# One branch in place of two around the last pair of experts

## The chip, the cores and the metric

The kernel runs on one core of one Trainium2 chip. The metric is the time of one execution on the device in microseconds (us), lower is better. The core has five engines, each with an instruction stream of its own: TensorE (PE in the profile, its weight loads PEld), VectorE (DVE), ScalarE (ACT), GpSimd (POOL) and SyncE (SP), which here only issues DMAs. The engines wait for each other through semaphores: every engine has a counter that its instructions raise, and others wait until it has reached a value.

## The reference

Two layers over 512 tokens of 1024 channels. Each layer is a mixer (layer 0: two convolution modules; layer 1: a gating unit and chunked attention), a layer norm, a mixture of experts and a second layer norm. The mixture is what matters here:

```python
# 32 experts (4 groups of 8); a token takes its best group, and the two best experts of it
expert_idx = g_idx * EXPERTS_PER_GROUP + e_idx          # (512, 2)
# each expert, on the tokens that chose it:
hb = jax.nn.silu(xb @ w_gate[e]) * (xb @ w_up[e])       # 1024 -> 512
y  = hb @ w_down[e]                                     # 512 -> 1024
# out: the two experts' results per token, weighted
```

How many tokens choose an expert depends on the data, so the kernel has code for every case and branches at run time over what isn't needed.

## The kernel before, in words

**Pairs.** `experts` (L977) goes over the 32 experts of a layer in 16 pairs (g = 0 to 15, L1056). A pair's tokens sit in 128 slots, 64 for each expert (or 96 and 32 in some pairs). For each pair PE computes the gate product (`proj2("g")`, L1063), ACT its Silu (`gated`, L755), PE the up product (`proj2("u")`, L1108), DVE the product of both (`hidden`, L760); PE transposes it and ACT copies the transposed tile `hT` to SBUF (`hidden_T`, L768); PE then computes the down product in two halves of 512 columns (`down`, L777, PSUM tiles `y0` and `y1`), from which ACT and DVE make two parts (L778, L779). The result of a pair is added to the tokens by `combine` (L789, L790 on PE, L798 on DVE) during the next pair. All expert products are issued by the helper line L745.

**Weights.** An expert has 6 MB of weights. SP streams them through eight large buffers ("units") and one more made of pieces, in an order fixed by `Stream` (L909): 2 MB matrices, each load waiting until PE has released the unit. The last pair's up and down weights are loaded as halves (L944, L947).

**Overflow.** Where an expert has more tokens than slots, two things can follow. `overflow` (L1079) handles a small excess of the pair with 128 slots more; it stands in a branch behind `hidden_T` (L1120, `tc.If(v > 0)`, v being the pair's count, loaded into registers at L1106 by all engines). `crowded` (L1031), the general loop, handles any number of tokens: for each of the 16 pairs it has a loop that gathers 64 tokens per expert, loads the six weight matrices into units (`slots`, L1032) and computes all of it. All 16 loops stand inside one branch (L1033, `tc.If(most > 0)`, most being the largest count of all pairs, loaded at L1128 at the end of pair 14). `crowded()` is called at the start of pair 15, ahead of its gate product (L1060).

An engine that doesn't enter a branch's body jumps over it, and then raises the semaphores by what the body would have raised them: these are the rows `EVENT_SEMAPHORE` of L1033 and L1120. Whoever uses a buffer after the branch that the body also uses waits for these raises. For PE alone a hint ahead of the branch (L1107, L1129) says which way it will go.

**After the branch of the last pair.** `last()` (L1061) is, in layer 0, `last0` (L1570): it loads the two 2 MB weights `val` and `v` of layer 1's mixer into units 7 and 3, which are also the two units that the general loop uses. `last2()` (L1124) is there `last0b` (L1575), which loads three more 2 MB weights and the 2 MB table TB behind it. In layer 1 `last()` is empty and `last2()` loads two rows of parameters. After the last pair's down halves follows `Last` (L800), which adds the result and takes the statistics of the layer norm.

Of the kernel before, what the change touches and what calls it, by code (L numbers as in the profile page):

```python
# [7 lines left out]
F32 = mybir.dt.float32  # L8
F32R = mybir.dt.float32r
BF = mybir.dt.bfloat16  # L10
I32 = mybir.dt.int32
AF = mybir.ActivationFunctionType
OP = mybir.AluOpType
AX = mybir.AxisListType
# [8 lines left out]
NP = NE // 2  # L23
# [3 lines left out]
COLS = [0, 1, 2, 3, 13, 4, 5, 12, 6, 7, 14, 8, 9, 15, 10, 11]  # L27
HEAVY = 12
NTHR = 6
WIDE = 3  # L30
# [13 lines left out]
def trunk(ctx: ExitStack, tc: tile.TileContext, a, out, layers=2, moe=True):  # L44
    nc = tc.nc
    PE, ACT, DVE, POOL = nc.tensor, nc.scalar, nc.vector, nc.gpsimd
# [3 lines left out]
    wk = ctx.enter_context(tc.tile_pool(name="wk", bufs=1))  # L50
# [3 lines left out]
    TT = DVE.tensor_tensor  # L54
# [11 lines left out]
    def small(shape, name, dt=F32, **kw):  # L66
        return wk.tile([128] + list(shape), dt, name=name, **kw)
# [374 lines left out]
    class Router:  # L442
# [178 lines left out]
        def counts(self):  # L621
            c = self.rk[:, NT]
            big = wk.tile([128, NE, NE], F32, name="big", tag="xb")
            TT(big, self.at, bc(c[:, None, :], [NE, NE]), op=OP.mult)
            cs = small([NP, 2], "cs", tag="rcb")
            DVE.tensor_reduce(cs.rearrange("p g two -> p (g two)"), big, axis=AX.X, op=OP.add)
            over = small([2, NP, 2], "over", tag="scr")
            for i in range(2):
                TT(over[:, i], cs, lim[:, i], op=OP.is_gt)
            nxs = small([2 * NP + 1], "nxs")  # L630
            n, m = nxs[:, 0:NP], nxs[:, NP:2 * NP]
            mxc = small([NP], "mxc", tag="mxc")
            DVE.tensor_reduce(mxc, over[:, 1], axis=AX.X, op=OP.max)
            DVE.scalar_tensor_tensor(n, over[:, 0, :, 1], 2.0, over[:, 0, :, 0], op0=OP.mult, op1=OP.add)
            DVE.scalar_tensor_tensor(n, mxc, float(WIDE), n, op0=OP.mult, op1=OP.max)
            mxe = small([NP], "mxe", tag="mxc")
            DVE.tensor_reduce(mxe, c.rearrange("p (g two) -> p g two", two=2), axis=AX.X, op=OP.max)
            nx = small([NP, NTHR], "nx", tag="scr")
            TT(nx, bc(mxe[:, :, None], [NP, NTHR]), bc(thr[:, None, :], [NP, NTHR]), op=OP.is_gt)
            DVE.tensor_reduce(m, nx, axis=AX.X, op=OP.add)  # L640
            for g in FIRST:
                DVE.scalar_tensor_tensor(m[:, g:g + 1], mxe[:, g:g + 1], float(CAP), m[:, g:g + 1], op0=OP.is_gt, op1=OP.add)
            DVE.tensor_reduce(nxs[:, 2 * NP:], m, axis=AX.X, op=OP.max)
            nxi = small([2 * NP + 1], "nxi", I32)
            DVE.tensor_copy(nxi, nxs)
            return nxi

# [99 lines left out]
    def proj2(tag, xt, wa, wb, own=EVEN[0]):  # L747
        p = ptile(tag)
        for k in range(KD):
            by_slots(p, xt[:, k], (wa[:, k], wb[:, k]), own, start=(k == 0), stop=(k == KD - 1))  # L750
        return p
# [6 lines left out]
    def hidden(sg, pu):  # L758
        h = wk.tile([128, 512], F32, name="h", tag="q1")
        DVE.tensor_mul(h, sg, pu)  # L760
        return h

    def hidden_T(h):
        p = mtile((128, 4, 128))
        for j in range(4):
            PE.transpose(p[:, j], h[:, j * 128:(j + 1) * 128], ident)  # L766
        hT = wk.tile([128, 4, 128], F32, name="hT", tag="q2")
        ACT.activation(hT, p, AF.Copy)  # L768
        return hT

# [11 lines left out]
    def onehot_S(tk, tag="q3"):  # L782
        S = wk.tile([128, T], F32R, name="S", tag=tag)
        TS(S, io, tk, None, op0=OP.is_equal)
        return S
# [6 lines left out]
    def combine(S, yh, yl, ts=range(NT)):  # L792
        for t in ts:
            for h in range(2):
                s = slice(h * 512, (h + 1) * 512)
                p = mtile()
                spread(p, S, yh, yl, t, h)
                DVE.tensor_add(acc[:, t, s], acc[:, t, s], p)  # L798
# [168 lines left out]
    ET = mybir.EngineType  # L967

    def count(nxi, i, **kw):
        return nc.values_load(nxi[0:1, i:i + 1], min_val=0, max_val=NTHR + 1,  # L970
                              skip_runtime_bounds_check_because="a count of blocks", **kw)

    def when(nxi, i, above, engines=None):
        v = count(nxi, i, **({} if engines is None else {"engines": engines}))
        return v, tc.If(v > above)

    def experts(rt, ws, T1, pt, x1d, xt, xg, xg2, update, last, last2, lead, finish):  # L977
# [52 lines left out]

        def crowded():  # L1031
            slots = ws.order[6:8]  # L1032
            with tc.If(most > 0, label=f"most{ws.l}", preferred_fallthrough_block=True):  # L1033
                for g in range(NP):
                    v, cond = when(nxi, NP + g, 0)
                    with cond:
                        cur = small([2, NT], "cur")
                        R3, yh, yl = (wk.tile([128, D], F32R, name="room", tag=t) for t in ("l1", "xt1", "lng"))
                        R3 = R3.rearrange("p (j t m) -> p j t m", j=2, t=NT)
                        TS(cur, rt.r, 0.0 if g in FIRST else -float(CAP), None, op0=OP.add)  # L1040
                        with tc.For_i(0, v, 1):
                            TS(cur, cur, -float(CAP), None, op0=OP.add)
                            rt.onehot(R3, range(NT), cur)
                            T3 = Table(rt, R3)
                            T3.one(2 * g)
                            gather(xg, x1d, T3.idx[:, 0:1])
                            xo = gather_T(xg, rt.gb, wk.tile([128, KD, 128], F32, name="xo", tag="xb"))
                            u = [ws.fetch(0, j, slots[j], g) for j in range(2)]
                            h3 = gated(proj2("g", xo, *u))
                            u = [ws.fetch(0, 2 + j, slots[j], g) for j in range(2)]  # L1050
                            h3 = hidden_T(hidden(h3, proj2("u", xo, *u)))
                            u = [ws.fetch(0, 4 + j, slots[j], g) for j in range(2)]
                            y3 = down(h3, *u, T3.wt[:, 0:1], (yh, yl))
                            combine(onehot_S(T3.tk[:, 0:1], "q2"), *y3)

        for g in range(NP):  # L1056
            W = lambda j: ws.u[6 * g + j]
            own, own2 = EVEN if COLS[g] < HEAVY else ODD
            if g == NP - 1:
                crowded()  # L1060
                last()  # L1061
            skip = f"skip{ws.l}_{g}"
            sg = gated(proj2("g", xt, W(0), W(1), own))  # L1063
            if g == 0:
# [14 lines left out]
            def overflow(v):  # L1079
                h2 = wk.tile([128, 512], F32, name="h2", tag="r")  # L1080
                xo = gather_T(xg2, rt.gb, wk.tile([128, KD, 128], F32, name="xo", tag="xb"))
                hT2 = wk.tile([128, 4, 128], F32, name="hT2", tag="q0")

                def wide():
                    ACT.activation(h2, proj8("g", xo, (W(0), W(1)), own2), AF.Silu)
                    DVE.tensor_mul(h2, h2, proj8("u", xo, (W(2), W(3)), own2))
                    hidden2_T(h2, hT2, 4)

                def single(e):
                    b = (0, 1) if own2 == EVEN[1] else (2, 1)  # L1090
                    s = slice(0, 128)
                    ACT.activation(h2[:, s], proj1("g", xo, W(e), b[e]), AF.Silu)
                    DVE.tensor_mul(h2[:, s], h2[:, s], proj1("u", xo, W(2 + e), b[e]))
                    hidden2_T(h2, hT2, 1)
                    r = slice(SUB * b[e], SUB * b[e] + SUB)
                    for i, src in enumerate((T2.tk, T2.wt)):
                        blocks4(tw, lambda o, c: DVE.tensor_copy(o[:, i:i + 1], col(src, g)[r]))
                either(v, wide, single)
                either(v, lambda: down8(hT2, (W(4), W(5)), col(T2.wt, g), col(T2.tk, g), own2),
                       lambda e: down1(hT2, W(4 + e), tw[:, 1:2], tw[:, 0:1]))  # L1100
# [2 lines left out]
                if g == NP - 1:  # L1103
                    combine(S, *prev, (0, 1))
            if g > 1:
                v = count(nxi, COLS[g])  # L1106
                tc.mark_branch_hint_location(skip, v > 0, engines=[ET.PE])  # L1107
            pu = proj2("u", xt, W(2), W(3), own)  # L1108
            h = hidden(sg, pu)
# [8 lines left out]
                combine(S, *prev, range(CM, NT))  # L1118
            if g > 1:
                with tc.If(v > 0, label=skip, preferred_fallthrough_block=True):  # L1120
                    overflow(v)
            ws.load(6 * g + 4 + 9)
            if g == NP - 1:
                last2()  # L1124
            if 0 < g < NP - 1:
                gather2(g + 1)
            if g == NP - 2:
                most = count(nxi, 2 * NP)  # L1128
                tc.mark_branch_hint_location(f"most{ws.l}", most > 0, engines=[ET.PE])  # L1129
            if g == NP - 1:  # L1130
                S = onehot_S(col(T1.tk, g))
            if g < NP - 1:
# [541 lines left out]
```

## Time and profile before

| | us |
|---|---|
| runs: median of 3 | 1455.97 |
| runs: lowest, highest | 1446.28, 1456.77 |
| the profiled execution, its own time | 1450.72 |
| the profiled execution, its span (first to last instruction) | 1448.9 |
| PE busy in the span | 1326.9 (92%) |
| DVE, ACT, POOL busy | 675.9, 368.3, 294.0 |
[...]

PE is busy nearly throughout, and the DMA queues move 420 GB/s and more while experts run, so two limits lie close together there. Layer 0's experts end and layer 1's mixer begins at about 700 us; layer 1's experts end at about 1430 us. A row of a group of instructions has its busy time, the mean of one in ns, the idle time of its engine just before, and what ended that idle time. A row of the timeline has the start, the length, the engine, the line, the operation, how many, and in brackets the idle time before it. Names that end in q (ACTq, DVEq, POOLq, SPq, PEldq) are instructions that the engine's sequencer handles by itself, such as branches and semaphore raises.

### The profile page before, as it was taken

Reading aid. Unit: us, or ns where it says so; the run is one execution under the profiler, and the core shown is the slowest. Engines: PE = TensorE matmul, PEld = TensorE weight load, DVE = VectorE, ACT = ScalarE, POOL = GpSimd, SP = SyncE. Lnnn points to the kernel's source line nnn. Section 1 sums busy time; section 2 is a strip of 40 time slices with the busy share of each in tenths; the row PEclk is TensorE's granted clock in tenths of the full one; section 3 lists DMA queues with packets and bytes.
Section 4 is the critical chain, followed back from the end, with each engine's and each line's share of the span. In section 5 each row is a group of like instructions: output and inputs, shape, how many; then the busy total and the mean of one; then the engine's idle time right before and its main releaser. Section 6 shows DMA issues by size and latency. Waiting matters only on the chain. (4 is left out here: it accounts for less than half of the span.)

```text
span 1448.9 us, 19205 instructions
## 1 busy us (share of the span) xinstructions
PE 1326.9 (92%) x7119; PEld 698.7 (48%) x7121; DVE 675.9 (47%) x1387; ACT 368.3 (25%) x694; POOL 294.0 (20%) x261
## 2 busy tenths in 40 slices
PE   9989999998978999988899999999998999988984
PEld 6767764343333433333576767744433343333331
DVE  7998588232222332232718555784322232322336
ACT  5545631111101111111524455521111111111101
POOL 5785610000000000000463229300000000000002
PEclk9999999999998999999999999999999999999997
DMA  7505479999997899999700018789999999999971
GB/s 293 232 5 241 166 262 425 420 424 422 420 400 301 355 426 423 422 420 378 283 1 1 23 66 325 268 320 423 421 423 424 423 423 422 425 421 422 420 304 59
DMA packets 56693, 461.19 MB, mean 318 GB/s; under 512 B 8661, under 2 KB 9301, under 8 KB 33089
## 3 DMA queue, kind: packets, MB, share of 16 engines
q1 hardware_dynamic: 51184, 449.96, 75.4%
q0 software_dynamic: 4464, 7.79, 1.5%
q8 instruction: 101, 1.65, 0.5%
q10 hardware_dynamic: 864, 1.13, 0.2%
q14 instruction: 80, 0.65, 0.1%
HBM read 461.04 MB, written 6.29 MB: 323 GB/s over the span
## 5 line engine op out<-in xcount | busy, mean ns | idle before, releaser
L745 PE MATMUL pu<-w,xt 128*64 128x512 f32 (+1 forms) x1280 | 247.8, 606 | 31.8 <-DMA w<-in_w_up_dram 31.8
L745 PE MATMUL py<-w,hT 128*64 128x512 f32 (+1 forms) x1280 | 242.3, 611 | 18.4 <-issue 7.3
L745 PE MATMUL pg<-w,xt 128*64 128x512 f32 (+1 forms) x1280 | 235.1, 600 | 10.9 <-ACTq L1033 10.9
L760 DVE TENSOR_TENSOR h<-sg,pu 128x512 f32<-128x512 f32 x32 | 22.0, 688 | 379.9 <-issue 342.7
L690 POOL DMA_INDIRECT xg<-x1d,idx x29 | 28.7, 990 | 794.3 <-PE m L439 711.6
L745 PEld LDWEIGHTS pu<-w,xt 128*64 128x64 f32 (+1 forms) x1280 | 75.4, 129 | 194.1 <-issue 149.0
L798 DVE TENSOR_TENSOR acc<-acc,m 128x512 f32<-128x512 f32 x240 | 148.6, 680 | 17.9 <-PE m L790 15.7
L745 PEld LDWEIGHTS pg<-w,xt 128*64 128x64 f32 (+1 forms) x1280 | 77.5, 127 | 163.4 <-issue 144.6
L745 PEld LDWEIGHTS py<-w,hT 128*64 128x64 f32 (+1 forms) x1280 | 71.7, 128 | 150.7 <-issue 146.8
L779 DVE SCALAR_TENSOR_TENSOR y<-py,wt,y 128x512 fp32r<-128x512 f32 x64 | 48.0, 750 | 194.6 <-ACT y L778 194.6
L778 ACT ACTIVATE y<-py,wt 128x512 fp32r<-128x512 f32 x64 | 44.0, 687 | 295.1 <-PE py L745 295.1
L789 PE MATMUL m<-y,S 128*128 128x512 f32 x248 | 106.2, 428 | 0.0
L109 POOL TENSOR_TENSOR wl<-win,wh 128x512 fp32r<-128x512 f32 x64 | 84.5, 1335 | 67.7 <-ACT wh L108 67.5
L790 PE MATMUL m<-y,S 128*128 128x512 f32 x248 | 97.8, 394 | 0.0
L768 ACT ACTIVATE hT<-m 128x512 f32<-128x512 f32 x32 | 19.1, 598 | 304.9 <-PE m L766 282.9
L109 POOL TENSOR_TENSOR wl<-wo,wh 128x512 fp32r<-128x512 f32 x64 | 82.3, 1314 | 34.8 <-ACT wh L108 34.4
L755 ACT ACTIVATE sg<-pg 128x512 f32<-128x512 f32 x32 | 19.1, 597 | 219.0 <-PE pg L745 219.0
L789 PEld LDWEIGHTS m<-y,S 128*128 128x128 f32 x248 | 46.6, 188 | 39.7 <-issue 26.9
L128 PE MATMUL m<-xh,wl 128*128 128x512 f32 x144 | 58.7, 408 | 3.1 <-POOL wl L109 3.1
L127 PE MATMUL m<-xh,wh 128*128 128x512 f32 x144 | 58.3, 405 | 0.8 <-ACT wh L108 0.8
L129 PE MATMUL m<-xl,wh 128*128 128x512 f32 x144 | 57.9, 402 | 0.0
L108 ACT ACTIVATE wh<-win 128x512 fp32r<-128x512 f32 x64 | 38.9, 625 | 49.0 <-PE pg L129 13.4
(445 smaller groups left out, 1858.8 us busy)
## 6 DMA issues: line engine op xcount, KB each, us to landing
w<-in_w_gate_dram SPq DMA_DIRECT2D x64, 2048.0 KB, 25.0
w<-in_w_up_dram SPq DMA_DIRECT2D x50, 2048.0 KB, 18.3
w<-in_w_down_dram SPq DMA_DIRECT2D x50, 2048.0 KB, 21.2
w<-in_w_up_dram SPq DMA_DIRECT2D x40, 512.0 KB, 24.7
w<-in_w_down_dram SPq DMA_DIRECT2D x40, 512.0 KB, 22.3
win<-in_w_in_dram SPq DMA_DIRECT2D x18, 512.0 KB, 7.6
wo<-in_w_out_dram SPq DMA_DIRECT2D x4, 2048.0 KB, 12.2
w<-in_w_up_dram SPq DMA_DIRECT2D x8, 1024.0 KB, 16.2
```

What stands on the lines that cost most here:

```text
L108: ACT.activation(h, src, AF.Copy)
L109: POOL.tensor_tensor(l, src, h, op=OP.subtract)
L127: PE.matmul(p, wh[:, j], xh[:, k], start=(k == 0), stop=False)
L128: PE.matmul(p, wl[:, j], xh[:, k], start=False, stop=False)
L129: PE.matmul(p, wh[:, j], xl[:, k], start=False, stop=(k == KD - 1))
L690: POOL.indirect_dma_start(out=dst, out_offset=None, in_=x1d, in_offset=bass.IndirectOffsetOnAxis(ap=idx_col, axis=0), bounds_check=T - 1, ...
L745: PE.matmul(p[w * c:w * c + w], x[:, w * c:w * c + w], ww[own[w * c // SUB]], **kw)
L778: ACT.activation(yh[:, s], p, AF.Copy, scale=wt)
L779: DVE.scalar_tensor_tensor(yl[:, s], p, wt, yh[:, s], op0=OP.mult, op1=OP.subtract)
L789: PE.matmul(p, S[:, t * 128:(t + 1) * 128], yh[:, s], start=start, stop=False)
L790: PE.matmul(p, S[:, t * 128:(t + 1) * 128], yl[:, s], start=False, stop=True)
L798: DVE.tensor_add(acc[:, t, s], acc[:, t, s], p)
```

## The change

The call of the general loop moves from the start of pair 15 into the body of that pair's overflow branch, behind the up product. The branch is now taken when either is needed: a 34th count, the sum of most and of the last pair's own count, is made on DVE in `counts` and loaded in place of the pair's own at L1106. Inside, each part has a branch of its own. The separate load of most at the end of pair 14, its hint, and the branch around the general loop ahead of the gate product go. Since `hT` of the last pair now lives across the general loop, the loop takes other buffers for its own hidden tile (`q3` in place of `q2`) and its one-hot matrix (`r` in place of `q2`). `last()` moves with the call, from ahead of the gate product to behind the branch.

```diff
@@ counts
-            nxs = small([2 * NP + 1], "nxs")
+            nxs = small([2 * NP + 2], "nxs")
...
-            DVE.tensor_reduce(nxs[:, 2 * NP:], m, axis=AX.X, op=OP.max)
-            nxi = small([2 * NP + 1], "nxi", I32)
+            DVE.tensor_reduce(nxs[:, 2 * NP:2 * NP + 1], m, axis=AX.X, op=OP.max)
+            TT(nxs[:, 2 * NP + 1:], nxs[:, 2 * NP:2 * NP + 1], n[:, COLS[-1]:COLS[-1] + 1], op=OP.add)
+            nxi = small([2 * NP + 2], "nxi", I32)
@@ hidden_T
-    def hidden_T(h):
+    def hidden_T(h, tag="q2"):
...
-        hT = wk.tile([128, 4, 128], F32, name="hT", tag="q2")
+        hT = wk.tile([128, 4, 128], F32, name="hT", tag=tag)
@@ count
-        return nc.values_load(nxi[0:1, i:i + 1], min_val=0, max_val=NTHR + 1,
+        return nc.values_load(nxi[0:1, i:i + 1], min_val=0, max_val=NTHR + 1 + WIDE,
@@ crowded
-            with tc.If(most > 0, label=f"most{ws.l}", preferred_fallthrough_block=True):
+            with when(nxi, 2 * NP, 0)[1]:
...
-                            h3 = hidden_T(hidden(h3, proj2("u", xo, *u)))
+                            h3 = hidden_T(hidden(h3, proj2("u", xo, *u)), "q3")
...
-                            combine(onehot_S(T3.tk[:, 0:1], "q2"), *y3)
+                            combine(onehot_S(T3.tk[:, 0:1], "r"), *y3)
@@ the loop over pairs
-            if g == NP - 1:
-                crowded()
-                last()
             skip = f"skip{ws.l}_{g}"
             sg = gated(proj2("g", xt, W(0), W(1), own))
...
-                v = count(nxi, COLS[g])
+                v = count(nxi, COLS[g] if g < NP - 1 else 2 * NP + 1)
                 tc.mark_branch_hint_location(skip, v > 0, engines=[ET.PE])
             pu = proj2("u", xt, W(2), W(3), own)
...
                 with tc.If(v > 0, label=skip, preferred_fallthrough_block=True):
-                    overflow(v)
+                    if g < NP - 1:
+                        overflow(v)
+                    else:
+                        v1, cond = when(nxi, COLS[g], 0)
+                        with cond:
+                            overflow(v1)
+                        crowded()
+                if g == NP - 1:
+                    last()
             ws.load(6 * g + 4 + 9)
...
-            if g == NP - 2:
-                most = count(nxi, 2 * NP)
-                tc.mark_branch_hint_location(f"most{ws.l}", most > 0, engines=[ET.PE])
```

## Rows read from the trace of the kernel before

**Rows 1.** The page's groups: line, operation xcount | busy, mean ns | idle before, releaser
```profile
L745 PE MATMUL pg<-w,xt 128*64 128x512 f32 (+1 forms) x1280 | 235.1, 600 | 10.9 <-ACTq L1033 10.9
```
**Rows 2.** Line 1033, both layers: operation xcount: ns min/median/max, first and last start
```profile
L1033 PEldq COMPARE_BRANCH  x2: 6067/6130/6194, 656.4 to 1383.9; - x2
L1033 ACTq COMPARE_BRANCH  x2: 45/45/45, 660.1 to 1387.6; - x2
L1033 ACTq EVENT_SEMAPHORE  x4: 17/17/17, 665.4 to 1393.1; - x4
L1033 SPq COMPARE_BRANCH  x2: 45/45/45, 668.5 to 1395.5; - x2
L1033 SPq EVENT_SEMAPHORE  x14: 17/17/17, 673.8 to 1405.0; - x14
```
**Rows 3.** Timeline, PE and ACT, last pair of layer 0 and then of layer 1
```profile
656.40 3.65 PE L745 MATMUL py<-w,hT 128*64 128x512 f32 x16
665.46 8.93 PE L745 MATMUL pg<-w,xt 128*64 128x512 f32 x32 [5.40 <-ACTq L1033]
676.38 7.09 PE L745 MATMUL pu<-w,xt 128*64 128x512 f32 x32
686.06 0.60 ACT L768 ACTIVATE hT<-m 128x512 f32<-128x512 f32 x1 [10.97 <-PEq L1120]
686.71 3.65 PE L745 MATMUL py<-w,hT 128*64 128x512 f32 x16 [0.74 <-ACTq L1120]
...
1393.08 8.64 PE L745 MATMUL pg<-w,xt 128*64 128x512 f32 x32 [5.54 <-ACTq L1033]
```
**Rows 4.** Timeline, PE, first down products of pairs 13 and 14 in layer 0
```profile
619.01 3.64 PE L745 MATMUL py<-w,hT 128*32 128x512 f32 x32
...
651.80 3.65 PE L745 MATMUL py<-w,hT 128*64 128x512 f32 x16 [0.80 <-PEq L1120]
```
**Rows 5.** Line 1120, last pair of layer 0, then all branches of PE and ACT
```profile
L1120 PEldq COMPARE_BRANCH  x1: 442/442/442, 684.9 to 684.9; - x1
L1120 ACTq COMPARE_BRANCH  x1: 45/45/45, 686.1 to 686.1; - x1
...
L1120 PEldq COMPARE_BRANCH  x28: 89/358/4182, 270.7 to 1412.3; - x28
L1120 ACTq EVENT_SEMAPHORE  x27: 17/17/17, 269.5 to 1414.0; - x27
```
**Rows 6.** Windows: A:B length, busy by engine, granted clock of PE, DMA share, GB/s
```profile
665.00:670.00 5.00, 4.54 (x14) 1.46 (x16) 0.48 (x1) 0.00 (x0) 0.00 (x0) 0.58 1.02 378
680.00:685.00 5.00, 5.00 (x25) 2.21 (x21) 1.42 (x3) 0.00 (x0) 0.00 (x0) 1.00 1.01 429
1405.00:1415.00 10.00, 9.26 (x46) 4.06 (x44) 3.56 (x6) 1.52 (x2) 0.00 (x0) 1.00 0.38 123
```
**Rows 7.** One load each, lines 964 (layer 1), 1573, 1331: issue, then us to landing
```profile
L964 SPq DMA_DIRECT2D w<-in_w_gate_dram x1: 333/333/333, 1362.2 to 1362.2; - x1
DMA to landing us min/median/max: 25.6/25.6/25.6
...
L1573 SPq DMA_DIRECT2D wval<-in_w_in1t_dram x1: 356/356/356, 675.2 to 675.2; - x1
DMA to landing us min/median/max: 9.8/9.8/9.8
...
L1331 SPq DMA_DIRECT2D row<-in_rows_dram x1: 363/363/363, 690.2 to 690.2; - x1
DMA to landing us min/median/max: 22.2/22.2/22.2
```
**Rows 8.** First readers of lines 1573's and 1331's loads: timeline ACT, then line 1360
```profile
698.36 1.14 ACT L108 ACTIVATE wh<-wval 128x512 fp32r<-128x512 f32 x2
...
L1360 DVE TENSOR_TENSOR val<-m,row x4: 673/684/692, 722.8 to 736.6; 128x512 f32<-128x512 f32 x4
```
**Rows 9.** Line 642 on DVE: a small operation of the shape of the added one
```profile
L642 DVE SCALAR_TENSOR_TENSOR nxs<-mxe,nxs x4: 152/156/159, 230.2 to 975.1; 128x1 f32<-128x1 f32 x4
```

## The prediction, made before the change was run

> **What bounds the kernel now.** I read the page's groups first. The gate product is idle ahead of itself for 10.9 us in all, and all of it is put down to ACT at line 1033, the branch around the general loop [rows 1]. With two layers that is some 5.4 us a layer, and it is the only thing that ever holds a gate product. Then I read line 1033 alone [rows 2]. The reader is to see that no engine goes into the body (each has a branch and then raises) and how far a branch and the first raise behind it lie apart: on ACT 660.1 to 665.4, on SP 668.5 to 673.8. Both take 5.3 us although the branch itself takes 45 ns; on PE the branch itself takes 6.07 and 6.19 us. So each engine pays this for itself, at full DMA load (share 1.02, [rows 6]). Third, the timeline of the last pair [rows 3]: the second down half of pair 14 ends at 656.40 + 3.65 = 660.05, and the gate product begins at 665.46, when ACT has raised its counter. PE's own branch was over by 656.4 + 6.07 = 662.5, so ACT's is the late one. [...] Fourth, line 1120, the overflow branch: the same jump, over a short body, costs ACT nothing that PE sees. In the last pair ACT's branch stands at 686.1 and PE goes on at 686.71, just after `hT` is copied (686.06 + 0.60 = 686.66) [rows 3, 5]. I read the 5.3 us as the fetch of instructions that aren't at hand after a long jump; that reading is a guess from the rows, the 5.3 us are not.
>
> Neither branch is taken in either layer's last pair: ACT makes 27 raises at line 1120 for 28 branches, the last at 1414.0, in layer 1's last pair [rows 5], and line 1033 has raises for both layers. The inputs are the same, so the sum of both counts is zero and the merged branch is skipped too.
>
> **The change part by part, layer 0.**
> (a) The load of most and its hint at the end of pair 14 go. They stand between PE's raise and its next weight load: PE is idle 0.80 us ahead of that pair's down product, in pair 13 too little to be shown [rows 4]. Minus 0.7 us.
> (b) The branch ahead of the gate product goes: minus 5.40 us of idle time [rows 3]. Late next would be the gate weights, but nothing held them here: the only releaser of gate products is line 1033 [rows 1].
> (c) With the stall goes the slow stretch behind it: 8.93 - 7.09 = minus 1.84 us [rows 3].
> (d) The merged branch has the general loop in its body, so it is the long jump that line 1033 was. PE's hint is for PE alone. ACT reaches the branch when it has issued `hT` (686.06 and 686.1 in the old times, [rows 3, 5]), and raises 5.3 us later. The down product writes `y0`, which the general loop's down product writes as well and ACT reads there; so PE must wait for that raise. Nothing covers it: between `hT` and the down product PE has no other work. Old: 686.71 - 686.06 = 0.65 us from `hT` to the down product. New: 5.25 to 5.4 for the jump (660.1 to 665.4, and 5.4 in layer 1 [rows 2]) and 0.08 for PE, 5.33. Plus 4.7 us. The bounds are 4.18 us, the longest that PE took at line 1120, and 6.19, its longest at line 1033 [rows 2, 5]; below stands also nothing at all, if the jump should find its target at hand (a rival). I take 5.3, the row of the same engine and the same body. PE's own branch, some 1.1 us ahead of `hT` (684.9 against 686.06), would end 5.0 us behind `hT` even if its hint came to nothing: not the later one.
> (e) The slow stretch then follows this stall, in the down product: plus 1.84, by (c).
> Sum: -0.7 - 5.4 - 1.84 + 4.7 + 1.84 = -1.4 us.
>
> **Layer 1.** The second gate weight was issued at 1362.2 and lands 25.6 us later, 1387.8 [rows 7]; so (a) gives nothing and the gate product starts at 1387.8 in place of 1393.08: -5.28 [rows 3]. (c) and (e) cancel again (8.64 - 7.09 = 1.55 each). (d) is +4.8, with 5.4 on ACT. Sum -0.5 us. By then the DMA queues are at a share of 0.38 (1405 to 1415, [rows 6]), which may shorten the fetch.
>
> [...] No run here shows a long jump over idle queues.
>
> **What costs nothing.** One operation more on DVE in each layer, 0.16 us by its neighbour [rows 9], in pair 0, where the first user of the counts is two pairs on; if it weren't covered, 0.3 us in all. The other tags: the general loop doesn't run. The one-hot matrix behind the branch takes `q3` and so waits for the raises too, but it is needed only after 3.65 us of down product. `last()` and `last2()`: SP reaches the old branch at 668.5 and the two loads go out at 675.2 [rows 2, 7]. SP still jumps from about 668.5 to 673.8, but units 7 and 3 are used by the general loop, whose raise on PE now comes with the merged branch: PE's branch moves from 684.9 to 684.9 - 7.9 = 677.0 (the sum of a to c), and with 6.1 us of jump the raise is at 683.2. The loads leave 8 us later, and everything behind them in a queue that is full (1.01 from 680 to 685, [rows 6]) moves by up to as much. Their readers: `val` landed at 675.2 + 9.8 = 685.0 and is first read at 698.36, later 693 against 697. The row of biases issued at 690.2 landed at 712.4 and is read at 722.8; later 720.4 against 721.4 [rows 7, 8]. So it just fits, with 1 us to spare at the worst, and I take nothing.
>
> **The sum.** -1.4 - 0.5 = -1.9 us. Against the profiled execution's own time, 1450.72 (span 1448.9 and 1.8 around it), that is 1448.8. The three timed runs went from 1446.28 to 1456.77 with a median 5.25 above the profiled one; the mean of these four is 1452.4, so for a new median I forecast 1452.4 - 1.9 = 1450.5.
>
> **Rivals.**
> First, the stall doesn't come back: the target of the merged jump is at hand, or the raise isn't waited for. For it: 27 jumps of ACT at line 1120 cost nothing. Against it: those bodies are short, and at line 1033 both engines shown, in both layers, paid at least 5.3 us. Then (d) and (e) fall away: -7.9 and -5.28 - 1.55 = -6.8, together -14.7: 1437.7, 1.0% less.
> Second, slower: the loads of `last()` are held so long that layer 1's mixer waits. That decides from the point where the row of biases lands after 721.4, that is, when the loads leave more than 9 us late. If SP pays a second jump of 5.3 us behind PE's raise, they leave at 683.2 + 5.3 = 688.5, 13.3 us late; the row lands at 725.7, 4.3 us after it is wanted, and the whole is 2.4 us slower: 1454.8. Against it: SP waits for nobody ahead of its own branch at line 1033, and jumps while PE is still busy.
> Third, layer 1's code lies elsewhere in memory, and PE's hinted branches, 0.36 us at the median and 4.18 once in 28 [rows 5], miss more often. Each miss costs up to 3.8 us; two of them make 1456.2.
> That the change doesn't do what it says would need a count above zero, which the rows exclude.
>
> **Chances and range.** Forecast 0.66, first rival 0.1, second 0.11, third 0.13. A measurement of this kernel tells about 1% (14.5 us) from no change. The first rival lies on that bound, so half of it is faster; the others are within. Since runs of one kernel here lie 10 us apart, I leave 0.03 for slower and 0.07 for faster. The range is the bounds of (d) in both layers (1448 to 1452), widened by the spread of runs, 5 us to either side, and by the second and third rival above and part of the first below: 1442 to 1459.
>
> **What would show it.** Right: in both layers the gate product of the last pair follows the down half with no idle time and takes 7.1 us; the down product stands idle some 5.4 us before it, put down to ACT at line 1120, and takes about 1.8 us longer than 3.65; ACT's branch and raise at line 1120 lie 5.3 us apart in the last pair; the loads of line 1573 leave at about 683. Wrong: no gap at line 1120 (first rival), a DMA or DVE `val` wait in layer 1's mixer (second), or PE branches of 4 us at other pairs of layer 1 (third).

## The result, and the profile after

The changed kernel takes 1444.61 us at the median of 20 runs (1440.08 to 1451.12), the kernel before 1454.05 us at the median of 20 runs beside it (1446.28 to 1457.83). The medians are 9.4 us apart and the means 7.7; the ratio taken from all these runs is 0.995, with an interval of 0.9936 to 0.9964: some 7 us faster, where 1.9 us were forecast. The profiled execution took 1445.25 us (span 1443.1). Run twice more, in other sessions, the same kernel gave 0.994 (0.9916 to 0.9964) and 0.9954 (0.9932 to 0.9976).

The page's groups come first; this line answers to [rows 1]:

```profile
L746 PE MATMUL pg<-w,xt 128*64 128x512 f32 (+1 forms) x1280 | 232.7, 594 | 0.1
```

The gate products, 10.9 us idle before, now never wait at their start. The wait has gone to the down product, and it is smaller. The timeline of PE at the last pair, layer 0 and then layer 1, answers to [rows 3] and, with its first line, to [rows 4]:

```profile
644.23 3.65 PE L746 MATMUL py<-w,hT 128*64 128x512 f32 x16
648.84 3.65 PE L746 MATMUL py<-w,hT 128*64 128x512 f32 x16
652.33 8.12 PE L746 MATMUL pg<-w,xt 128*64 128x512 f32 x32
662.43 7.09 PE L746 MATMUL pu<-w,xt 128*64 128x512 f32 x32
675.71 5.35 PE L746 MATMUL py<-w,hT 128*64 128x512 f32 x16 [3.68 <-DVEq L1118]
...
1382.95 8.13 PE L746 MATMUL pg<-w,xt 128*64 128x512 f32 x32
...
1406.56 5.35 PE L746 MATMUL py<-w,hT 128*64 128x512 f32 x16 [3.89 <-DVEq L1118]
```

Three things are to be seen. The gate product follows pair 14's down product at once in both layers. It takes 8.12 us, 1.03 more than the up product. The down product stands idle 3.68 and 3.89 us ahead of itself, not 5.4, and what releases it is DVE at the merged branch (now L1118), not ACT; then it runs 1.70 us longer than the 3.65 of its kind.

Who jumps how long is seen at line 1118 alone, in layer 0 and in layer 1. These answer to [rows 2] and [rows 5]: a branch and the first raise behind it are one engine's jump.

```profile
L1118 PEldq EVENT_SEMAPHORE  x2: 51/51/51, 672.1 to 672.2; - x2
L1118 ACTq EVENT_SEMAPHORE  x2: 17/17/17, 674.9 to 675.0; - x2
L1118 DVEq EVENT_SEMAPHORE  x2: 21/21/21, 675.4 to 675.5; - x2
...
L1118 PEldq COMPARE_BRANCH  x1: 342/342/342, 671.0 to 671.0; - x1
L1118 DVEq COMPARE_BRANCH  x1: 56/56/56, 671.6 to 671.6; - x1
L1118 ACTq COMPARE_BRANCH  x1: 45/45/45, 672.1 to 672.1; - x1
...
L1118 ACTq EVENT_SEMAPHORE  x2: 17/17/17, 1405.7 to 1405.8; - x2
L1118 DVEq EVENT_SEMAPHORE  x2: 21/21/21, 1406.3 to 1406.4; - x2
...
L1118 DVEq COMPARE_BRANCH  x1: 56/56/56, 1402.3 to 1402.3; - x1
L1118 ACTq COMPARE_BRANCH  x1: 45/45/45, 1402.7 to 1402.7; - x1
```

ACT's jump took 2.9 and 3.0 us, DVE's 3.8 and 4.0; before, at line 1033, ACT's took 5.3 and 5.4 [rows 2] and DVE's 5.6 and 5.5. PE's branch took 0.34 us, where the one at line 1033 had taken 6.07. The windows around the jump show what else differs (columns as in [rows 6]):

```profile
670.00:672.00 2.00, 2.00 (x11) 1.45 (x9) 2.00 (x4) 0.00 (x0) 0.00 (x0) 1.00 0.19 71
672.00:674.00 2.00, 0.03 (x1) 0.00 (x0) 0.72 (x2) 0.60 (x1) 0.00 (x0) 1.00 0.74 157
676.00:680.00 4.00, 4.00 (x12) 1.36 (x10) 0.25 (x1) 0.57 (x2) 0.00 (x0) 0.57 1.00 414
1401.00:1403.00 2.00, 1.67 (x10) 1.16 (x8) 2.00 (x4) 0.29 (x1) 0.00 (x0) 1.00 0.13 49
1403.00:1405.00 2.00, 0.00 (x0) 0.00 (x0) 0.36 (x1) 0.30 (x1) 0.00 (x0) 1.00 0.09 28
```

and those of the kernel before around its jumps at line 1033:

```profile
660.00:665.00 5.00, 0.06 (x2) 0.00 (x0) 0.75 (x1) 0.69 (x1) 0.00 (x0) 0.74 1.00 399
1388.00:1393.00 5.00, 0.00 (x0) 0.00 (x0) 0.75 (x1) 0.30 (x1) 0.00 (x0) 0.98 1.01 391
```

Before, the jump fell where the DMA engines were busy without a gap (shares 1.00 and 1.01). Now it falls where the stream of weights has just ended: the share is 0.13 to 0.19 when it begins, and 0.09 in the next two microseconds of layer 1. The 0.74 from 672 on in layer 0 are the loads of `last()`, which set out at 672.2, when the jumps had begun; from 672 to 673 alone the share is 0.17. The window from 676 has a granted clock of 0.57: part of the down product ran at the lower of the two levels that the traces show, 0.50 of full speed from 677 to 679 alone. Behind the stall of the kernel before it was 0.50 from 664 to 666.

**Where the time went.** One stretch holds all of the change: from the start of ACT's copy of pair 14's `hT` to the start of the second `y` of the last pair. By the timelines it took 49.55 us in layer 0 and 49.38 in layer 1 before, and takes 47.18 and 47.40 now: 4.4 us less. The other two profiles of the changed kernel give 46.13 and 47.42, 47.47 and 45.55, so 5.2 us less on average of the three. That is less than the 6.7 to 8.7 us that the three ratios say; the rest is taken up behind the experiments.

### The profile page after: what moved, and what is told of

The parts are those of the page before. It is cut to its first block, busy times and chain, and to the rows that moved or that the text cites. A ratio compares the mean times of both kernels' runs of the same rounds, so it can differ in the third digit from the quotient of the medians.

```text
span 1443.1 us, 19168 instructions
## 1 busy us (share of the span) xinstructions
PE 1331.4 (92%) x7121; PEld 703.9 (49%) x7121; DVE 678.4 (47%) x1389; ACT 368.2 (26%) x694; POOL 294.1 (20%) x261
## 3 DMA queue, kind: packets, MB, share of 16 engines
q8 instruction: 97, 1.59, 0.4%
## 5 line engine op out<-in xcount | busy, mean ns | idle before, releaser
L746 PE MATMUL pu<-w,xt 128*64 128x512 f32 (+1 forms) x1280 | 251.1, 625 | 28.6 <-DMA w<-in_w_up_dram 28.6
L108 ACT ACTIVATE wh<-win 128x512 fp32r<-128x512 f32 x64 | 38.9, 624 | 48.7 <-PE pg L129 13.6
```

What stands on the lines that cost most here:

```text
L108: ACT.activation(h, src, AF.Copy)
L746: PE.matmul(p[w * c:w * c + w], x[:, w * c:w * c + w], ww[own[w * c // SUB]], **kw)
```

## The experiments

The theory: a long jump fetches its target over the DMA queues, and is shorter now only because the weights no longer fill them at that place. The first rival: the way over the merged branch is shorter for some other reason (another place in memory, say), whatever the queues do. The second: the fetch isn't the matter, moving or merging is, by the semaphores or the hint that it spares.

**The kernel before, once more** (no edit), for the scatter.

> The kernel before once more, unchanged. If the two traces compared so far stand for their kernels, the gate product of the last pair stands idle 5.3 to 5.6 us in both layers again, and the stretch from hT of pair 14 to the first y of the last pair is 42.0 to 42.2 us. The overflow that runs in pair 8 tells what is chance: if PE's branch inside it (3.97 us in one trace, 0.83 in the other) belongs to the kernel it is 4.0 again, if it is chance it may be anything from 0.8 to 4.

It took 1455.54 us (12 runs) beside 1450.53 (32 runs), a ratio of 1.002 (1.0002 to 1.0038). Two copies of one text can thus differ by 0.2%, and by 5 us between their medians, with an interval that leaves out 1; the last pairs are the same to 0.3 us (49.38 and 49.65), and the gate product stood idle 5.47 and 5.35 us again. A difference of 3 us between two kernels need not come from their texts.

**The changed kernel, once more** (no edit).

> The changed kernel once more, unchanged. Expected from its first trace: 3.6 to 3.9 us of idle time ahead of the last pair's down product, 39.8 to 40.1 us from hT of pair 14 to the first y of the last pair. The slow operation in layer 1's router (4.72 us at line 472, 0.77 before) is there again if it belongs to the change, and gone if it is a chance meeting of DVE and POOL. Time against before: ratio 0.995, that is 5 to 9 us less.

1443.41 us (9 runs), 0.994 (0.9916 to 0.9964). The down product waited 3.73 and 3.89 us, and ACT's jumps took 3.09 and 3.01: the short jump is no accident of one profile. In layer 0 the gate product took 7.04 us this time, not 8.12, and the stretch is a microsecond shorter than expected for it. The slow operation at line 472 was there again (4.45 us), but the kernel before had it too in its second profile (4.73).

**Queues filled again at the jump.** To the changed kernel, two 2 MB loads into units that lie free, just ahead of the merged branch in SP's stream; nobody reads them:

```diff
+                if g == NP - 1:
+                    for s in ws.order[6:8]:
+                        nc.sync.dma_start(unit(s, [128, 8, 512], F32, "busy"), a["w_gate"][0])
                 with tc.If(v > 0, label=skip, preferred_fallthrough_block=True):
```

> The changed kernel, with two more 2 MB loads into the two free units on SP's queue just ahead of the merged branch, in both layers, so that the DMA queues are still full while the engines jump. Theory (the jump is a fetch through the DMA queues, and got shorter because they had drained): ACT's branch and raise lie 5.2 to 5.7 us apart in place of 2.9, and the down product is idle 5.2 to 5.7 us in place of 3.7 to 3.9. Rival (the merged branch jumps a shorter way, or the target is partly at hand): 2.9 and 3.7 as in the changed kernel. In layer 0 the loads of the next mixer land some 10 us later, which may cost up to 5 us there.

The loads run across the jump. The merged branch (L1121 there) in layer 0:

```profile
L1121 DVEq EVENT_SEMAPHORE  x2: 21/21/21, 683.3 to 683.4; - x2
L1121 ACTq EVENT_SEMAPHORE  x2: 17/17/17, 683.5 to 683.5; - x2
...
L1121 DVEq COMPARE_BRANCH  x1: 56/56/56, 677.4 to 677.4; - x1
L1121 ACTq COMPARE_BRANCH  x1: 45/45/45, 677.9 to 677.9; - x1
```

the window in which the jump starts:

```profile
676.00:678.00 2.00, 1.82 (x10) 1.27 (x9) 2.00 (x5) 0.14 (x1) 0.00 (x0) 1.00 1.00 423
```

and the down product in the timeline of PE:

```profile
683.54 6.34 PE L746 MATMUL py<-w,hT 128*64 128x512 f32 x16 [5.72 <-ACTq L1121]
```

With the DMA share back at 1.00 the jump of ACT is back at 5.6 us and DVE's at 5.8, and the wait at 5.72 (5.66 in layer 1). The ratio is 1.0009 (0.999 to 1.0028): the gain is gone. The time alone wouldn't prove it, since the two loads also hold up those of the next mixer (in layer 0 these leave at 685.4, not 672.2); the stretches do, 98.66 us together against 98.93 before. Only loads on SP were added, none of the branch's code moved to another place in the order, so the first rival falls. This is also what the prediction had summed up, made to happen: with a jump of 5.3 us the change is worth next to nothing.

The fetches can be seen in the traces as packets of an instruction queue, q14, of 8 KB each. This is the queue's row (packets, MB, share) in the DMA views of three windows: 663.4 to 665.0 in the kernel before, 672.5 to 674.5 in the changed one, 681.2 to 682.1 with the queues filled:

```profile
q14 instruction: 2, 0.02, 2.5%
...
q14 instruction: 2, 0.02, 3.1%
...
q14 instruction: 2, 0.02, 5.4%
```

The trace doesn't name the engine of a packet, but in all three the raises of ACT and DVE come 1.4 and 1.6 us behind the ends of the two. The packets take 0.3 to 0.6 us themselves. What differs is when they start: before, 3.5 us behind ACT's branch and 3.7 behind DVE's; in the changed kernel 0.9 and 1.8; with the queues filled 3.8 and 3.9. So in these windows a long jump loses its extra time ahead of the packet, while other loads fill the DMA engines.

**The hint for ACT and DVE too**, in the last pair of the changed kernel:

```diff
-                tc.mark_branch_hint_location(skip, v > 0, engines=[ET.PE])
+                tc.mark_branch_hint_location(skip, v > 0, engines=[ET.PE] if g < NP - 1 else [ET.PE, ET.Activation, ET.DVE])
```

> The changed kernel, with the hint of the last pair's branch also on ACT and DVE. Theory (a fetch, started only when the branch is met): the count is loaded on ACT 11.5 us and on DVE 9 us ahead of their branches, more than any fetch seen, so both raise at once and the idle time of 3.7 to 3.9 us and the slow down product behind it (5.35 in place of 3.65) go in both layers: 2 x 5 = some 10 us less than the changed kernel, ratio to before 0.987 to 0.990. Rival (the wait is something else than a fetch): no change against the changed kernel.

1446.19 us (12 runs), 0.9967 (0.995 to 0.9984); the gain expected of a hint that helps isn't there. No change against the changed kernel is what the expectation named for a wait that isn't a fetch; the packets above speak for a fetch all the same. Both engines do execute a hint (DVE at 667.8, ACT at 665.8), some 9 and 11 us ahead of their branches, and then jump as long as without it. Line 1118 in layer 0:

```profile
L1118 ACTq EVENT_SEMAPHORE  x2: 17/17/17, 679.6 to 679.7; - x2
L1118 DVEq EVENT_SEMAPHORE  x2: 21/21/21, 680.2 to 680.3; - x2
...
L1118 DVEq COMPARE_BRANCH  x1: 74/74/74, 676.4 to 676.4; - x1
L1118 ACTq COMPARE_BRANCH  x1: 64/64/64, 676.9 to 676.9; - x1
```

and the down product in the timeline, layer 0 and layer 1:

```profile
680.51 5.35 PE L746 MATMUL py<-w,hT 128*64 128x512 f32 x16 [3.69 <-DVEq L1118]
...
1409.16 3.65 PE L746 MATMUL py<-w,hT 128*64 128x512 f32 x16 [3.10 <-DVEq L1118]
```

2.7 us on ACT, 3.8 on DVE. The trace has no fetch that the hints started: between them and the branches the instruction queues move no packet more than in the changed kernel (three there, from 661.0 to 671.6), and the two packets of the jumps start 1.0 and 1.7 us behind the branches in layer 0, much as there (0.9 and 1.8). Why a hint does nothing on these engines stays open. Layer 1's wait of 3.10 us had no slow stretch behind it (3.65 in place of 5.35); the one of 3.16 us in the third run of the changed kernel had (below), so the length of the wait alone doesn't tell.

**The loop's branch behind the gate product, in the kernel before.** Both branches stay; the gate product of pair 15 is only issued ahead of the loop's branch, and the loop computes its own gate in another PSUM tile. The jump remains under full queues (a DMA share of 0.98 to 1.00), but with 7 us of work above it:

```diff
-                            h3 = gated(proj2("g", xo, *u))
+                            h3 = gated(proj2("y1", xo, *u))
...
-            if g == NP - 1:
-                crowded()
-                last()
             skip = f"skip{ws.l}_{g}"
-            sg = gated(proj2("g", xt, W(0), W(1), own))
+            pg = proj2("g", xt, W(0), W(1), own)
+            if g == NP - 1:
+                crowded()
+                last()
+            sg = gated(pg)
```

> Keeps the two branches of the kernel before, but issues the last pair's gate product ahead of the general loop's branch instead of behind it (the loop's own gate product goes to another PSUM buffer). If the long jump costs ACT and DVE what instruction fetches cost beside full DMA queues (5.3 to 5.7 us in the last run with loads in the way), it now lies under a gate product of some 7 us: the idle time of TensorE ahead of the gate product falls from 5.4 to under 1 us in both layers, the one ahead of the up product rises by at most 2 us, no stretch at a lower clock follows, and the stretch from pair 14's transposed tile to the end of the last pair falls from 49.5 to about 43 us per layer; ratio to the kernel before about 0.990. If instead the wait only changes its place (TensorE itself misses its own jump, since its hint comes too near, or the combine's inputs become late), 4 to 6 us of idle time stand ahead of the up product and the stretch stays at 47 to 49 us; ratio 0.997 to 1.000.

1438.93 us (6 runs), 0.9899 (0.987 to 0.9929). The timeline of PE in layer 0:

```profile
658.34 7.04 PE L745 MATMUL pg<-w,xt 128*64 128x512 f32 x32
665.87 0.47 PE L789 MATMUL m<-y,S 128*128 128x512 f32 x1 [0.49 <-DVE S L784]
```

and line 1033 there:

```profile
L1033 ACTq EVENT_SEMAPHORE  x2: 17/17/17, 664.2 to 664.2; - x2
L1033 DVEq EVENT_SEMAPHORE  x2: 21/21/21, 665.0 to 665.1; - x2
...
L1033 ACTq COMPARE_BRANCH  x1: 45/45/45, 658.6 to 658.6; - x1
L1033 DVEq COMPARE_BRANCH  x1: 56/56/56, 659.3 to 659.3; - x1
L1033 PEldq COMPARE_BRANCH  x1: 3123/3123/3123, 660.9 to 660.9; - x1
```

The jumps are as long as ever, 5.6 us on ACT and 5.7 on DVE, and all that PE waits for them is the 0.49 us ahead of the combine (0.45 in layer 1). Layer 0's down product has a gap of 1.09 us ahead of its last matmul (1.24 in the repeat below), which no other kernel here shows; its reason stays open. The stretches are 44.28 and 43.05 us. This is the better version of the two: it hides the jump, where the change moves it to a place without cover. **Run again, word for word, beside the changed kernel:**

> The kernel with the loop's branch behind the gate product once more, word for word, beside the changed kernel on one chip. If its gain of 14.9 us is the two stalls with their slow stretches (11.6 us by the stretches at the last pairs) and the rest is scatter, the ratio lies between 0.988 and 0.994, no idle time over 1 us stands ahead of the gate product or the up product of the last pair, and the two stretches are 43 to 44.5 us. If the gain was a lucky placing of other jumps, the ratio is over 0.995.

1442.61 us (6 runs), 0.9927 (0.9899 to 0.9955), with stretches of 44.41 and 42.97 us and no wait over 1 us ahead of the gate or the up product.

**Moved but not merged.** The changed kernel with two branches behind the up product:

```diff
-                    if g < NP - 1:
-                        overflow(v)
-                    else:
-                        v1, cond = when(nxi, COLS[g], 0)
-                        with cond:
-                            overflow(v1)
-                        crowded()
+                    overflow(v)
                 if g == NP - 1:
+                    crowded()
                     last()
```

The count of most and a hint for it are loaded beside the pair's own count and hint.

> The changed kernel with its merged branch taken apart again: behind the up product first the last pair's own overflow branch on its own count, then the general loop's branch with its hint. If moving the loop's branch is what gives the gain and merging adds little, the time stays within 3 us of the changed kernel, the stretch from pair 14's transposed tile to the end of the last pair is 0.7 to 1 us longer per layer than there (about 48 us), and TensorE waits 4.4 to 4.8 us ahead of the down product. If merging is what gives the gain, two jumps in a row cost ACT and DVE twice the 2.9 to 3.9 us, the wait ahead of the down product grows to 6.5 us or more, and the stretch is back at 49 us or more.

1452.73 us (12 runs), 0.9989 (0.9968 to 1.001): no gain, and stretches of 50.23 and 50.54 us. Neither theory had the reason. Line 1121 (the own branch) in layer 0:

```profile
L1121 PEldq COMPARE_BRANCH  x1: 3424/3424/3424, 676.8 to 676.8; - x1
```

line 1034 (the loop's):

```profile
L1034 ACTq EVENT_SEMAPHORE  x2: 17/17/17, 681.0 to 681.1; - x2
L1034 DVEq EVENT_SEMAPHORE  x2: 21/21/21, 681.5 to 681.6; - x2
...
L1034 PEldq COMPARE_BRANCH  x1: 2957/2957/2957, 680.4 to 680.4; - x1
```

and the timeline of PE:

```profile
683.95 5.94 PE L746 MATMUL py<-w,hT 128*64 128x512 f32 x16 [6.14 <-PEq L1034]
```

ACT and DVE are done by 681.6; PE is late, because both of its branches missed, 3.42 and 2.96 us one after the other, though both had a hint. **So the same with one hint**, the loop's taken out:

```diff
-                    tc.mark_branch_hint_location(f"most{ws.l}", most > 0, engines=[ET.PE])
```

> The split kernel of the last run with one line less: TensorE's hint for the general loop's branch is gone, the one for the last pair's own branch stays. If two hints outstanding at once spoil each other, the own branch takes TensorE 0.3 to 0.4 us again (3.4 and 3.8 in the split kernel), its miss at the loop's branch (3 to 4 us) lies beside those of ACT and DVE, the idle time ahead of the down product falls from 6.1 and 6.9 to 4 to 4.8 us, and the stretch from pair 14's transposed tile to the end of the last pair to 48 to 48.7 us; the gain of merging is then 0.7 to 1.3 us a layer. If the missing hint is not the reason and two jumps in a row are the price, the own branch still takes TensorE over 3 us and the stretch stays at 50 us.

The own branch (L1120 there) in layer 0:

```profile
L1120 PEldq COMPARE_BRANCH  x1: 342/342/342, 676.0 to 676.0; - x1
```

the loop's branch:

```profile
L1034 PEldq COMPARE_BRANCH  x1: 3913/3913/3913, 677.2 to 677.2; - x1
```

and the down product:

```profile
681.77 5.83 PE L746 MATMUL py<-w,hT 128*64 128x512 f32 x16 [4.74 <-PEq L1034]
```

The own branch is back at 0.34 us, PE's one miss lies beside those of ACT and DVE, and the wait falls to 4.74 (4.86 in layer 1): 1446.68 us (7 runs), 0.9957 (0.9933 to 0.9982). The stretches are 47.61 and 49.43, where 48 to 48.7 were expected. Merging spares the wait some 1 us a layer, and the second hint, which would otherwise have to go too. How the gain divides isn't settled: by the ratio moving alone gives most of it (0.9957 against 0.995), by the stretches 1.9 of 5.2 us.

**The loop's branch behind the gate product, its count beside pair 14's own and no hint:**

```diff
+            if g == NP - 2:
+                most = count(nxi, 2 * NP)
             if g > 1:
                 v = count(nxi, COLS[g])
...
-            if g == NP - 2:
-                most = count(nxi, 2 * NP)
-                tc.mark_branch_hint_location(f"most{ws.l}", most > 0, engines=[ET.PE])
```

> The kernel with the loop's branch behind the gate product, its count loaded at pair 14 beside that pair's own count and without TensorE's hint. If the hint issued some 4.7 us ahead had done part of the fetch there, TensorE's jump takes 5.3 to 6.2 us now (3.1 and 4.4 with it) and the combine behind the gate product starts 0.8 to 1.5 us later, while the idle time ahead of pair 14's second half of the down product (0.8 us) goes: the stretch to the end of the last pair stays within 0.8 us of 44.3 and 43.1, and the time within 3 us. If the hint did nothing there, TensorE's jump is as before and the stretch is some 0.7 us shorter per layer.

A miss for the stretch, a hit for the jump. PE's jump took 5.98 and 6.18 us without the hint, against 3.12 and 4.38 (and 2.61 and 3.94 in the repeat) with it, so the hint had done part of the work there, although it stood 10.8 us ahead and not 4.7 as the expectation says. The combine was idle 1.93 and 1.36 us ahead of itself, the wait at pair 14 went in both layers, as expected, and in layer 0 PE's own branch, hinted 9.9 us ahead, took 5.85 us, so that the down product waited 5.14 us and the stretch was 51.19 us; layer 1's was 43.99. The ratio is 0.9982 (0.9956 to 1.0008), with runs from 1439.37 to 1456.30.

**The changed kernel a third time** (no edit), for the part of the gain outside the last pairs.

> The changed kernel a third time. If the last pairs alone make its gain (4.9 us by the stretches), the ratio is 0.996 to 0.998 and the rest of the 7 to 9 us measured so far was scatter; if some other part of the program is quicker with it as a rule, the ratio is 0.993 to 0.996 again, the overflow that runs in pair 8 takes 29 to 30 us again instead of 35 to 37, and the stretches at the last pairs are 46 to 47.5 us.

1446.08 us (12 runs), 0.9954 (0.9932 to 0.9976), with waits of 3.96 and 3.16 us ahead of the down product (5.35 us long in both). The ratio is that of the second case, but the overflow in pair 8 took 35.99 us in this profile, from its `hT` to its `y`, so the place named there is not the reason. The table sets the change of the two stretches together, against 98.93 us, beside the change of time (ratio less 1, times 1453 us):

| kernel | stretches, us | their change | change of time, by the ratio |
|---|---|---|---|
| before, again | 99.03 | +0.1 | +2.9 |
| changed | 94.58 | -4.4 | -7.3 |
| changed, again | 93.55 | -5.4 | -8.7 |
| changed, third | 93.02 | -5.9 | -6.7 |
| queues filled | 98.66 | -0.3 | +1.3 |
| hint on ACT and DVE | 90.99 | -7.9 | -4.8 |
| split | 100.77 | +1.8 | -1.6 |
| split, one hint | 97.04 | -1.9 | -6.2 |
| behind the gate | 87.33 | -11.6 | -14.7 |
| behind the gate, again | 87.38 | -11.6 | -10.6 |
| behind the gate, no hint | 95.19 | -3.7 | -2.6 |

The two columns differ by -4.3 to +3.1 us without order, and by +2.8 where no line was changed; a stretch is that of one profile, a time that of several runs. So the last pairs are what the edits move, and some 2 to 3 us of the changed kernel's gain can't be told from scatter; no run settles whether all of it is.

## Why the prediction was right or wrong

The forecast, no change that a measurement of 1% could tell, and its range held. The size did not: 1.9 us were forecast, some 5 us came in the last pairs. The step that failed is one term, (d). That the range held owes something to luck: 1444.61 lies outside the 1448 to 1452 that the bounds of (d) had given, and inside 1442 to 1459 by the 5 us added for the spread of runs.

**(a) and (b), the count and the branch ahead of the gate product:** right in kind. Pair 14's down product has no idle time [rows 4] and the gate product no stall. But "late next would be the gate weights, but nothing held them here" was wrong for layer 0. The waits of PE's weight loads around the gate product say so:

```profile
PEld pg L746 <- DMA w<-in_w_gate_dram: 0.9, 1, 0.9
```

The second gate weight now lands inside the product, in both layers. In layer 1 the prediction had counted on that from its landing at 1387.8 [rows 7], though as a later start. In both it takes back what (a) had given. In the other two profiles of the changed kernel only one of the two gate products waits (8.18 and 8.15 us), the other takes 7.04.

**(c), the slow stretch behind the stall:** it went. The 8.12 us that the gate product still takes are that wait, not the clock, which is granted at 1.00 from 652.33 to 660.45.

**(d), the merged branch as the long jump of line 1033 (+4.7 us):** this term failed, by its size. That the stall would come back, behind `hT` and ahead of the down product, was right; from `hT` at 672.1 to the product are 3.6 us, where 5.33 were forecast and 0.65 were there before, so (d) is +3.0 us in layer 0 and some +3.2 in layer 1. Even the bound set below, 4.18 us, was too high. The price of 5.3 us had been read at a DMA share of 1.0 and was carried to a place where the share is 0.1 to 0.2. The prediction noted that for layer 1 ("which may shorten the fetch") and gave it no number. For layer 0 it read the row of 1.01 from 680 to 685 as a full queue [rows 6]. But in the kernel before, the stream of weights thins out ahead of that, as this window shows:

```profile
674.00:676.00 2.00, 2.00 (x9) 1.42 (x8) 0.92 (x2) 0.60 (x1) 0.00 (x0) 1.00 0.52 198
```

What fills the queue behind it are the loads of `last()`, out at 675.2 [rows 7], and these the change itself moves behind PE's raise, as the prediction says too. The run with the queues filled put 5.6 to 5.8 us back, and so names the cause. The direction that the prediction gave for layer 1 is right: its jumps, at a share of 0.09 to 0.13, measure 3.0 us (ACT) and 4.0 (DVE), where 5.4 was taken. The late one was DVE, which the prediction left out: it reaches the branch 0.4 us ahead of ACT and jumps a microsecond longer, its packet being the second of the two in layer 0.

**(e), the slow stretch behind it:** right, 1.70 us for 1.84.

Summed for layer 0: -0.8 - 5.4 - 0.8 (8.93 to 8.12) + 3.0 + 1.7 = -2.3 us, and the stretch measures -2.4. For layer 1: -0.8 - 5.5 - 0.5 + 3.2 + 1.7 = -1.9, and it measures -2.0.

**The rivals.** The first (no stall) is what lies under the gate product: the branch in the cover of another product gave 10.6 to 14.7 us, near the 14.7 worked out for it, though not by the change. The second didn't come. The loads of `last()` answer to [rows 7]:

```profile
L1576 SPq DMA_DIRECT2D wval<-in_w_in1t_dram x2: 356/559/762, 672.2 to 672.7; - x2
```

They left 3 us earlier than before and not 8 later. PE's raise, for which they waited, came at 672.1, since PE's hint, which had done nothing 4.7 us ahead of line 1033, worked at its new place (0.34 us); the prediction had priced that jump at 6.1. The third didn't come either: in layer 1 the longest PE branch at line 1118 took 0.45 us. But such misses do occur in other kernels here: with the loop's branch behind the gate product PE's overflow branch of one middle pair of layer 1, at 1126 to 1132 us, took 6.07 to 6.16 us in all three profiles, and with the split and one hint two such branches took 3.85 and 3.35. The rival's price was added up wrongly: two misses of 3.8 us on 1450.5 make 1458.1, not 1456.2, which is still inside the range.

That a jump has to do with DMA queues at all is read from the traces alone: two of the queues there are of the kind instruction, q14 moves the two packets above ahead of the raises of ACT and DVE, and the hint stands in the trace as BRANCH_PREFETCH_HINT (on PE at 657.4 us). One of the two instruction queues of the changed kernel moves 1.59 MB in 97 packets, 16.4 KB each; the other, to which the packets at ACT's and DVE's jumps belong, half of that a packet, 0.65 MB in 79:

```profile
q8 instruction: 97, 1.59, 0.4%
...
q14 instruction: 79, 0.65, 0.1%
```

What decides that an engine fetches, no run shows. What the jumps took, the runs do: 2.5 to 4.1 us on ACT and DVE where the weights had ended, 5.2 to 5.9 where loads filled the queues.

## What to carry to other kernels

A skipped branch over a long body cost ACT and DVE 2.5 to 5.9 us here, and its price is a matter of the place: read the DMA share there as it will be after the change, not as it is at the place from which the price was taken. Better than to move such a jump to a cheaper place is to issue the longest independent product ahead of it: the full price of 5.6 us then cost PE 0.5. And count the hints that are under way at once before adding a branch: where two were, here, both of PE's branches missed (3.42 and 2.96 us, against 0.34 with one).

## What the runs showed of the hardware

- A skipped long branch took ACT and DVE 5.2 to 5.9 us at a DMA share near 1.0, and 2.5 to 4.1 us where the share was 0.1 to 0.3 as the jump began. In the three windows above the difference lies ahead of the instruction queue's packet (0.9 and 1.8 us behind the branch, against 3.5 to 3.9 at full queues), which itself takes 0.3 to 0.6 us.
- With a hint 12.7 to 13.6 us ahead PE's jump over the long body took 0.34 to 0.36 us, with the queues filled too; without one it took 6.0 and 6.2 us at full queues and 3.9 and 4.1 at nearly empty ones. 4.7 us ahead a hint did nothing (6.07 and 6.19 us), 10.8 us ahead part of the work (2.6 to 4.4); but the short branch's came to 0.43 to 0.45 us at 9.8 to 9.9 us five times and to 5.85 once, so distance isn't all. For ACT and DVE it did nothing (2.7 and 3.8 us with it).
- Two hints under way at once: both of PE's branches missed, in both layers (3.42 and 2.96 us, 3.83 and 3.27); with one of them gone, the other held (0.34 and 0.36). The run took one hint out, so that the two spoil each other is shown for this pair alone.
- Two operations elsewhere vary by microseconds from profile to profile of one text: a branch inside pair 8's overflow takes PE 0.4, 0.8 or 3.8 us in the three profiles of the changed kernel, and a small DVE product in layer 1's mixer (L472) 0.77 us in one profile of the kernel before and 4.73 in the other. They are a part of the scatter.
